# The low part of the second half of every weight piece on GpSimd instead of VectorE

## The chip, the cores and the metric

The kernel runs on one core of one Trainium2 chip. The metric is the device time of one execution in microseconds (us), the median over several runs. Five engines work side by side, each in the order of its own queue: TensorE (PE in the profile, with its weight loads as PEld), VectorE (DVE), ScalarE (ACT), GpSimd (POOL) and SyncE (SP), which here only issues DMAs.

## What is computed

The reference is two transformer-like blocks in float32 over 256 tokens of width 1024. The first block has four layers: a Fourier mixer, a grouped-query attention, a dilated attention and a Fourier mixer again, each with an input projection, a gate, an attention over 256 memory tokens, an output projection and a layer norm. The second block has two layers; each has an RMS norm, a mixer of three parts (a gated unit, a state-space part, a low-rank attention), an output projection, another RMS norm and an MLP with 4096 hidden units.

```python
proj = jnp.matmul(h, w_in_a[j])                # a 1024 x N projection in each layer
y = jnp.matmul(y.astype(h.dtype), w_out[i])
h = layer_norm(DEEPNORM_ALPHA * h + y, ln_g[i], ln_b[i])
...
x = x + mix @ w_out[l]
x = x + squared_relu_mlp(rmsnorm(x, norm_mlp_g[l]), mlp_w1[l], mlp_w2[l])
```

## The kernel before, in words

All weights lie in one array of 380 pieces of 128 partitions by up to 1024 columns, in the order of their use (`plan`, L30). A piece is loaded by SP into one of four `raw` buffers (`load_raw`, L117). Every float32 operand of a matrix product is split into a high part, rounded to the type fp32r, and a low part, the difference from it; a product is three matmuls (high by high, high by low, low by high; `Group.add`, L212). The weights are split on the fly, half a piece at a time (`split_w`, L149): ACT rounds the half into `wh` (L158), then VectorE subtracts it from `raw` into `wl` (L160). There are 12 buffers for `wh` halves and 12 for `wl` halves, so the split can run up to six pieces ahead of the matmuls; `W` (L177) asks for it two pieces ahead in the program. The manual dependence at L163 to L166 keeps a half behind the half two before it; since the halves alternate, that is the same half of the piece before.

The order of the instructions on each engine is set by a planner that goes by dependences, by the place in the program and by `high_priority`. Two hand-written orders matter. `late` (set at L345) and `tail_of_chain` (L142) put some low parts behind the last instruction of a norm on VectorE, `normed`: `issue_after` queues what is issued on the engine of that instruction behind it, and only that. The norms themselves run from the sum into `x` (L623, L1295, L1429) over statistics (L414, L419, or ACT's squares at L355) to two small POOL instructions (L289 and L290 in `rsqrt`, L360 and L361 in `rms_x`), then back to VectorE (L423 and L425, or L369) and by PE transposes (L298) into the halves `xTh` and `xTl` (L189, L190) that feed the next projections. The two halves of the tokens (`hf`) go through this one after the other.

Apart from the norms, POOL adds the two products of the rotary embedding (L200), makes the low part of the gated branch (L197), and issues a few DMAs (L686, L695, L910, L914).

Of the kernel before, what the change touches and what calls it, by code (L numbers as in the profile page):

```python
# [9 lines left out]
F32 = mybir.dt.float32  # L10
# [3 lines left out]
ALU = mybir.AluOpType  # L14
# [56 lines left out]
def used(key):  # L71

    return 512 if key.startswith("dftt") else width(key)
# [3 lines left out]
def kernel(ctx: ExitStack, tc: tile.TileContext, x_in, wall, vec, tabs, small, out, dbg=None):  # L77
    nc = tc.nc
    V, A, G, PE = nc.vector, nc.scalar, nc.gpsimd, nc.tensor
# [23 lines left out]
    def pt(shape, dt=F32):  # L103
        return ab.tile(shape, dt, tag="P", name="pt", bufs=4)
# [37 lines left out]
    def tail_of_chain():  # L142
        late["skip"] -= 1
        if late["skip"] < 0 and late["n"] > 0:
            late["n"] -= 1
            return tc.issue_after(late["after"])
        return ExitStack()

    def split_w(n):  # L149
        key, _ = order[n]  # L150
        w, t = used(key), raws.pop(n)
        cut = w // 2
        hs, ls = [], []
        for c in (slice(0, cut), slice(cut, w)):
            k = c.stop - c.start
            h = wp.tile([P, PC // 2], F32R, tag="wh", name="wh", bufs=NW)
            l = wp.tile([P, PC // 2], F32R, tag="wl", name="wl", bufs=NW)
            ih = A.copy(out=h[:, :k], in_=t[:, c]).ins  # L158
            with tail_of_chain():
                il = V.tensor_tensor(out=l[:, :k], in0=t[:, c], in1=h[:, :k].bitcast(F32), op=ALU.subtract).ins  # L160
            splits.append((ih, il))

            if len(splits) > HOLD:  # L163
                for i, before in zip((ih, il), splits[-1 - HOLD]):
                    tc.add_manual_dep(i, before.name, mybir.DependencyInfo(
                        mybir.DependencyClass.Sync, mybir.DependencyReason.DATA))  # L166
            hs.append(h)
            ls.append(l)
        wts[n] = (Halves(hs, cut), Halves(ls, cut))
# [7 lines left out]
    def W(key, i, ahead=AHEAD):  # L177
        n = where[(key, i)]
        while state["split"] <= min(n + ahead, len(order) - 1):
            while state["raw"] <= min(state["split"] + 1, len(order) - 1):  # L180
                load_raw(state["raw"])
                state["raw"] += 1
            split_w(state["split"])
            state["split"] += 1
        return wts[n]
# [258 lines left out]
    for i in range(4):  # L444
# [3 lines left out]
        for c in range(2):  # L448
            for kk in range(2):
                k = 2 * i + kk  # L450
# [467 lines left out]
    for hf in range(2):  # L918
        t = pt([P, 512])
# [13 lines left out]
    def ph2(shape, dt=F32R):  # L933
        return p2.tile(shape, dt, tag="ph2", name="ph2", bufs=12)
# [503 lines left out]
    for hf in range(2):  # L1438
        t = [ph2([P, 512], F32) for _ in range(2)]
# [3 lines left out]
        for b in range(2):  # L1443
            c = slice(b * 512, (b + 1) * 512)
# [169 lines left out]
```

## Time and profile before

| what | value |
|---|---|
| three runs | 1343.18 us median (1342.47 to 1346.27) |
| the profiled execution | 1345.01 us, span 1343.3 us |
| PE busy | 1281.3 us, 95% |
| VectorE busy | 981.2 us, 73% |
| ScalarE busy | 759.9 us, 57% |
| GpSimd busy | 179.3 us, 13% |
| mean granted TensorE clock | 0.979 of full speed |

A busy time counts every stretch in which the engine works on at least one instruction; the ends of matmuls are modelled. An idle time is put down to what ended it.

### The profile page before, as it was taken

The page shows a single profiled execution, that of the slowest core. Times are in us where ns is not written, and L with a number is a line of the kernel's source. Part 1 is how long each engine was busy: PE and PEld are TensorE (multiplying, and loading weights), DVE is VectorE, ACT ScalarE, POOL GpSimd, SP SyncE. Part 2 cuts the span into 40 slices and gives each one's busy share as a digit, 9 for nine tenths or more (in the row PEclk, how much of TensorE's full clock was granted, in tenths as well). Part 3 has the DMA queues.
Part 4 walks back from the last instruction along what each step waited for, and adds up shares of the span by engine and source line. Part 5 has one row for each costly group of instructions (what it writes and reads, how often), then busy time and mean ns, then how long its engine had stood idle before and what let it go on. Part 6 is the DMA issues. An engine that isn't in the chain of part 4 may idle for free. (4 is left out here: it accounts for less than half of the span.)

```text
span 1343.3 us, 21990 instructions
## 1 busy us (share of the span) xinstructions
PE 1281.3 (95%) x7620; PEld 1103.7 (82%) x7620; DVE 981.2 (73%) x1990; ACT 759.9 (57%) x1691; POOL 179.3 (13%) x290
## 2 busy tenths in 40 slices
PE   8999989899999999998998989999999998999997
PEld 6987868588788878897987887889898896789896
DVE  7788977788777777777777896765556897665654
ACT  5664576655555655663654784555454774554543
POOL 1132401111112111123032201000001201000000
PEclk9999999999899999998998998999999998999999
DMA  8574523354344434455554542565554552466561
GB/s 290 180 224 138 170 85 100 105 189 155 104 125 151 156 111 127 147 168 168 183 179 155 180 135 80 169 204 181 187 183 148 158 166 81 141 206 187 187 187 51
DMA packets 64063, 209.55 MB, mean 156 GB/s; under 512 B 8520, under 2 KB 10192, under 8 KB 63952
## 3 DMA queue, kind: packets, MB, share of 16 engines
q1 hardware_dynamic: 60480, 203.33, 47.8%
q0 software_dynamic: 1888, 3.15, 0.8%
q10 hardware_dynamic: 1584, 1.67, 0.4%
q8 instruction: 60, 0.98, 0.3%
q14 instruction: 51, 0.42, 0.1%
HBM read 204.97 MB, written 2.10 MB: 154 GB/s over the span
## 5 line engine op out<-in xcount | busy, mean ns | idle before, releaser
L160 DVE TENSOR_TENSOR wl<-raw,wh 128x512 fp32r<-128x512 f32 (+4 forms) x760 | 504.9, 690 | 195.9 <-ACT wh L158 191.2
L158 ACT CAST wh<-raw 128x512 fp32r<-128x512 f32 (+4 forms) x760 | 443.6, 606 | 299.9 <-issue 77.9
L217 PE MATMUL acc<-wh,ph 128*128 128x512 f32 (+2 forms) x672 | 224.2, 390 | 5.3 <-DVE pt L1315 1.7
L217 PE MATMUL acc<-wh,xTh 128*128 128x512 f32 (+3 forms) x560 | 218.8, 392 | 2.9 <-ACT xTh L189 1.3
L217 PE MATMUL acc<-wl,xTh 128*128 128x512 f32 (+3 forms) x560 | 217.5, 389 | 3.6 <-DVE wl L160 3.6
L217 PE MATMUL acc<-wh,xTl 128*128 128x512 f32 (+3 forms) x560 | 216.7, 389 | 3.3 <-DVE xTl L190 3.3
L217 PEld LDWEIGHTS acc<-wh,ph 128*128 128x128 f32 x672 | 125.9, 190 | 33.8 <-ACT ph L189 2.9
L217 PE MATMUL acc<-wl,ph 128*128 128x512 f32 (+2 forms) x336 | 131.2, 391 | 0.0
L217 PEld LDWEIGHTS acc<-wh,xTl 128*128 128x128 f32 x560 | 107.4, 192 | 24.0 <-DVE xTl L190 5.9
L217 PE MATMUL tp<-xTl,wh 128*128 128x256 f32 x448 | 126.6, 283 | 0.0
L217 PE MATMUL tp<-xTh,wl 128*128 128x256 f32 x448 | 126.6, 283 | 0.0
L217 PE MATMUL tp<-xTh,wh 128*128 128x256 f32 x448 | 126.6, 283 | 0.0
L217 PEld LDWEIGHTS acc<-wh,xTh 128*128 128x128 f32 x560 | 107.5, 192 | 22.5 <-ACT xTh L189 2.9
L217 PEld LDWEIGHTS acc<-wl,xTh 128*128 128x128 f32 x560 | 107.7, 192 | 21.7 <-DVE wl L160 4.3
L217 PE MATMUL sc<-wh,ph 128*128 128x512 f32 (+1 forms) x328 | 104.2, 369 | 0.0
L217 PE MATMUL acc<-xTh,wh 128*128 128x256 f32 x336 | 97.2, 290 | 0.0
L217 PE MATMUL acc<-xTh,wl 128*128 128x256 f32 x336 | 96.6, 288 | 0.0
L217 PE MATMUL acc<-xTl,wh 128*128 128x256 f32 x336 | 96.1, 286 | 0.0
L200 POOL TENSOR_TENSOR t<-t,t 128x256 f32<-128x256 f32 (+3 forms) x84 | 54.3, 672 | 244.6 <-DVE t L716 214.9
L217 PEld LDWEIGHTS tp<-xTl,wh 128*128 128x128 f32 x448 | 85.7, 191 | 0.5
L217 PEld LDWEIGHTS tp<-xTh,wh 128*128 128x128 f32 x448 | 85.5, 191 | 0.6
L217 PEld LDWEIGHTS tp<-xTh,wl 128*128 128x128 f32 x448 | 85.7, 191 | 0.0
(272 smaller groups left out, 2169.8 us busy)
## 6 DMA issues: line engine op xcount, KB each, us to landing
raw<-in_wall_dram SPq DMA_DIRECT2D x338, 512.0 KB, 4.1
raw<-in_wall_dram SPq DMA_DIRECT2D x20, 384.0 KB, 3.6
ph<-in_vec_dram SPq DMA_DIRECT2D x20, 256.0 KB, 6.5
raw<-in_wall_dram SPq DMA_DIRECT2D x8, 422.0 KB, 3.5
gn<-in_vec_dram SPq DMA_DIRECT2D x5, 512.0 KB, 4.7
raw<-in_wall_dram SPq DMA_DIRECT2D x6, 288.0 KB, 3.2
raw<-in_wall_dram SPq DMA_DIRECT2D x6, 256.0 KB, 3.0
x<-in_x_in_dram SPq DMA_DIRECT2D x2, 512.0 KB, 7.9
```

Source lines behind the costliest of these rows:

```text
L158: ih = A.copy(out=h[:, :k], in_=t[:, c]).ins
L160: il = V.tensor_tensor(out=l[:, :k], in0=t[:, c], in1=h[:, :k].bitcast(F32), op=ALU.subtract).ins
L200: G.tensor_tensor(out=out, in0=a, in1=b, op=ALU.add)
L217: done[0] = PE.matmul(out=self.out, lhsT=s, rhs=m, start=(i == 1), stop=(i == bk["n"]), skip_group_check=True).ins
```

## The change

The low part of the second half of a piece (`c.start` is not 0) is issued on GpSimd (`G`), that of the first half stays on VectorE (`V`). Operands, buffers and manual dependences stay as they are. There are 380 pieces, so 380 of the 760 subtractions move.

```diff
             ih = A.copy(out=h[:, :k], in_=t[:, c]).ins
             with tail_of_chain():
-                il = V.tensor_tensor(out=l[:, :k], in0=t[:, c], in1=h[:, :k].bitcast(F32), op=ALU.subtract).ins
+                il = (G if c.start else V).tensor_tensor(
+                    out=l[:, :k], in0=t[:, c], in1=h[:, :k].bitcast(F32), op=ALU.subtract).ins
             splits.append((ih, il))
```

## Rows read from the trace of the kernel before

**Rows 1.** Busy time, share of the span and instructions of each engine.

```profile
PE 1281.3 (95%) x7620; PEld 1103.7 (82%) x7620; DVE 981.2 (73%) x1990; ACT 759.9 (57%) x1691; POOL 179.3 (13%) x290
```

**Rows 2.** PE's waits: engine, line, waited for: us in total, times, longest.

```profile
PE sc L298 <- DVE pt L369: 5.6, 2, 3.7
PE sc L886 <- POOL t L200: 4.7, 2, 2.4
PE tp L528 <- DVE PTl L190: 4.5, 2, 2.2
PE acc L217 <- DVE wl L160: 3.8, 3, 3.4
PE sc L298 <- DVE x L425: 3.3, 3, 1.6
PE acc L217 <- DVE xTl L190: 3.3, 5, 0.9
...
PE pv L217 <- DVE PTl L190: 2.2, 6, 0.9
...
PE acc L217 <- DVE pt L1315: 1.7, 2, 1.0
...
PE acc L217 <- ACT ph L539: 1.4, 1, 1.4
...
PE tp L528 <- DVE pt L574: 1.2, 2, 0.6
```

**Rows 3.** Stretches: length, busy (instructions) PE, PEld, DVE, ACT, POOL, clock, DMA.

```profile
617.00:727.00 110.00, 99.41 (x584) 86.97 (x583) 83.47 (x157) 56.55 (x137) 27.61 (x43) 0.92 0.52 163
...
857.00:1024.00 167.00, 167.00 (x1047) 150.13 (x1045) 95.83 (x148) 84.23 (x150) 0.12 (x1) 1.00 0.59 185
```

**Rows 4.** Waits of ACT and of SP's queue for the weight pieces.

```profile
ACT wh L158 <- PE acc L217: 76.6, 76, 5.9
...
ACT wh L158 <- DMA raw<-in_wall_dram: 23.8, 16, 4.8
...
SPq L121 <- DVE wl L160: 956.7, 313, 24.3
```

**Rows 5.** VectorE's groups by shape: the commonest low part; busy, mean ns.

```profile
L160 DVE TENSOR_TENSOR wl<-raw,wh 128x512 fp32r<-128x512 f32 x676 | 462.2, 710 | 181.5 <-ACT wh L158 177.4
```

**Rows 6.** POOL's timeline: start, us; two-input instructions at 85, 256 and 818 us.

```profile
85.26 5.80 POOL L197 TENSOR_TENSOR ph<-sg,ph 128x256 fp32r<-128x256 f32 x5
...
256.35 1.43 POOL L197 TENSOR_TENSOR ph<-sg,ph 128x256 fp32r<-128x256 f32 x2 [15.09 <-ACT ph L539]
...
818.60 1.00 POOL L200 TENSOR_TENSOR y<-y,pt 128x384 f32<-128x384 f32 x1 [16.91 <-DVE pt L1279]
```

**Rows 7.** VectorE's timeline beside the first of those rows.

```profile
86.93 1.23 DVE L160 TENSOR_TENSOR wl<-raw,wh 128x512 fp32r<-128x512 f32 x1
```

**Rows 8.** Timelines of POOL, VectorE and ACT in the norm of 705 to 713 us.

```profile
705.18 0.53 POOL L289 TENSOR_SCALAR st<-st 128x1 f32<-128x1 f32 x1 [15.73 <-DVE st L419]
705.79 0.95 POOL L290 TENSOR_TENSOR st<-st,mhalf 128x1 f32<-128x1 f32 x1
...
706.90 1.41 DVE L425 SCALAR_TENSOR_TENSOR x<-x,st,ph 128x512 f32<-128x512 f32 x2
711.44 1.41 DVE L369 SCALAR_TENSOR_TENSOR pt<-x,st,gn 128x512 f32<-128x512 f32 x2 [3.13 <-POOL st L361]
...
705.18 3.41 ACT L158 CAST wh<-raw 128x422 fp32r<-128x422 f32 x5 [0.15 <-PE acc L217]
```

**Rows 9.** VectorE's timeline in the norm of 613 to 617 us.

```profile
614.84 0.69 DVE L160 TENSOR_TENSOR wl<-raw,wh 128x512 fp32r<-128x512 f32 x1
615.45 0.75 DVE L425 SCALAR_TENSOR_TENSOR x<-x,st,ph 128x512 f32<-128x512 f32 x1
616.11 0.69 DVE L160 TENSOR_TENSOR wl<-raw,wh 128x512 fp32r<-128x512 f32 x1
616.71 0.75 DVE L425 SCALAR_TENSOR_TENSOR x<-x,st,ph 128x512 f32<-128x512 f32 x1
```

**Rows 10.** The page's group of POOL's rotary additions.

```profile
L200 POOL TENSOR_TENSOR t<-t,t 128x256 f32<-128x256 f32 (+3 forms) x84 | 54.3, 672 | 244.6 <-DVE t L716 214.9
```

## The prediction

> **What bounds the kernel now.** I read the engines' busy times first: PE is busy for 1281.3 of 1343.3 us [rows 1]. What an edit on VectorE or POOL can win is therefore in the 62 us in which PE stands still; what it can lose has no such limit. Next come PE's waits, which say who ended those pauses. No single wait is large: VectorE's last multiplication of a norm (L369) 5.6 us, its low parts of attention weights 4.5 and 2.2 us, the rotary sums of POOL 4.7 us, and the low parts of the weights, the ones that the edit touches, 3.8 us in three places out of 760 [rows 2]. So PE almost never waits for a low part. The reason is in the split's own waits: ACT waited 76 times, 76.6 us in all, until PE's accumulations gave a weight buffer back, and only 16 times for a load [rows 4]. The split mostly runs as far ahead as the buffers let it. The stretches show where the pauses are: in the MLP from 857 to 1024 us PE is busy throughout, in the crossing from one block to the other (617 to 727 us) it is idle for 10.6 of 110 us [rows 3]. The end of a norm is where a few microseconds on VectorE, ACT or POOL become microseconds of the whole. A change to the low parts must be judged there.
>
> **The change part by part.**
>
> *What VectorE gives away.* 380 subtractions leave it. One takes 0.69 us undisturbed [rows 9] and 0.71 on average [rows 5]; the instructions start 0.6 us apart when they follow each other (614.84, 615.45) [rows 9]. That is 380 x 0.6 = 228 us less for an engine that is busy 73% of the time. It is off PE's path nearly everywhere, so by itself it brings little; what it can bring is in the rows of PE's waits that end on VectorE in the middle of a stage (4.5 + 2.2 + 1.7 + 1.2 = 9.6 us) [rows 2]. These chains run through ACT and PE too, so I take a third, **-3 us**; bounds 0 and -9.6.
>
> *What POOL takes on.* No low part of 512 columns has run there. Two subtractions of 256 columns took 1.43 us, 0.72 each, and one addition of 384 columns 1.00 us [rows 6]. 128 columns more cost 0.28, so 512 should take about 1.28 us, and 380 of them at most 486 us. POOL goes from 179 us [rows 1] to some 660, half the span; it is no bound by its sum. Per piece PE is busy for 1281.3 / 380 = 3.4 us, POOL for 1.28 more than now.
>
> *What the two engines do to each other.* This is the term that speaks most against the change. From 85.26 us POOL made five subtractions of 256 columns in 5.80 us, 1.16 each instead of 0.72 [rows 6], and beside them a low part on VectorE took 1.23 us instead of 0.69 [rows 7, 9]. Each held the other up: the rows read as two instructions that take turns at reading two SBUF operands. VectorE lost 0.54 us to a subtraction of 256 columns; with 256 more at 0.28 per 128 that is 0.54 + 0.56 = 1.10 us for one of 512. The Trainium skill (SBUF — State Buffer, "Who interferes with whom") states that a VectorE instruction with two SBUF inputs contends with a GpSimd instruction that reads SBUF, and that the loser waits for the whole instruction; the trace agrees on the contention, not on the whole instruction, since 0.54 is less than 0.72. By the page a hit would cost 1.28 instead of 1.10, which would add 1 us to the sum below.
>
> *The norms.* PE's work crosses seven norms between layers: after each of the four first layers, after both mixers of the second block and between its two layers. In each, the first half of the tokens has PE waiting at once. Three things happen.
> (a) The two small POOL instructions (705.18 and 705.79) come when VectorE has the statistics [rows 8]. In just that time ACT rounds weights, five halves from 705.18 on [rows 8], and every second one now calls POOL for 1.28 us. Whoever comes in between waits for what is left, half of it on average, 0.64 us. The order that keeps low parts behind a norm acts on VectorE's queue alone, so POOL's low parts are not held back. 7 x 0.64 = **+4.5 us**; lower bound 0, upper 14 half norms x 1.28 = 18.
> (b) L423, L425 and L369 read two SBUF operands (`x` with the weights of the norm). A layer norm has four of them per half, an RMS norm two. I count two hits in each of the four layer norms and one in each of three RMS norms, 11 hits of 0.55 us, half of 1.10: **+6.1 us**; lower bound 0, upper 7 x 3 low parts x 1.10 = 23, since five halves on ACT bring at most three to POOL.
> (c) A low part stands between the instructions of the chain: at 614.84, which runs while VectorE would wait anyway, and at 616.11, which doesn't [rows 9]. Where the second kind is a second half it goes: 7 x 0.6 = **-4.2 us**; bounds 0 and twice that.
>
> *POOL's other work.* The 84 rotary additions, in 42 pairs [rows 10], and the low parts of the branch queue behind weights. PE already waits for POOL's sums twice, 4.7 us, and once for the branch [rows 2]. There each delay shows at once: 3 x (0.64 + 0.44, the contention of the rows above) = **+3.3 us**. Lower bound 0; if every pair were late by 0.64 with no cover, 27. A low part on POOL that waits for ACT, as on VectorE (177.4 us of idle time before it [rows 5]), also holds back POOL's DMAs at the end of the dilated layer (L910, L914); their data are wanted a layer later, which hides it.
>
> *Loads.* SP waits for the last reader of a `raw` buffer, 313 times a low part [rows 4]. The second half now frees it 1.28 - 0.69 = 0.59 us later. Where the split is far ahead this is hidden; if that cover is gone, each load costs 0.59. ACT waited for a load 16 times [rows 4], at the start and just behind norms: 16 x 0.59 = 9.4 as the upper bound, 0 as the lower; most loads there wait for the transfers of their neighbours, so I take **+2 us**. The broadcasts of norm weights in SP's queue move by the same 0.59, ahead of a need that is several pieces away.
>
> *The MLPs.* PE stood still for nothing there and POOL was empty (0.12 us of work) [rows 3]: 0.
>
> Sum: -3 + 4.5 + 6.1 - 4.2 + 3.3 + 2 = **+8.7 us**. The profiled execution took 1345.0 us, so 1353.7; it lies 1.8 us above the median of the three runs, and against that median the forecast is **1352 us**. About 0.3% (4 us) is what a measurement of this kernel can tell from no change.
>
> **The rivals.**
> *VectorE is the better for it.* Its place is the norm and the attention chains: fewer low parts in VectorE's queue, and POOL's are done early because nothing holds them back, so behind a norm VectorE has two halves to make where it had four. For it: eight of the waits of PE shown end on VectorE, 5.6 + 4.5 + 3.8 + 3.3 + 3.3 + 2.2 + 1.7 + 1.2 = 25.6 us [rows 2]. Against: the contention in the rows above takes back more than it gives (1.10 against 0.6 us) wherever the two meet. Price: with a third of the 25.6 us won and (a), (b) and POOL's delays near nothing, 1343.2 - 8.5 = 1335 us. It decides where a hit is met in fewer than half the norms, so that what leaves the chain outweighs what is put in its way. Chance 0.20.
> *All is hidden.* The split is ahead, PE is never without work, and gains and losses at the norms cancel: 1343 us. For it: 3.8 us of waits for 760 low parts. Against: the norm chain, where nothing is ahead. Chance 0.18.
> *POOL's queue becomes the wait.* The planner puts a low part between the two small instructions of a norm, as the low parts stand between the instructions of VectorE's chain [rows 9], and rotary sums come late in most groups. Price: (a) with both a rest and a whole low part, 7 x (0.64 + 1.28) = 13.4 instead of 4.5, and 10 us more from rotary sums, half of their upper bound less what is counted: 1352 + 8.9 + 10 = 1371 us. The granted clock, 0.92 of 2.4 GHz in the crossing with pauses against 1.00 in the MLP [rows 3], would fall with longer pauses. Chance 0.17.
> That the edit does nothing is excluded: `c.start` is 0 for the first slice alone.
>
> **How the numbers follow.** The forecast has a chance of 0.45. Slower by over 0.3%: 0.45 + 0.17 = 0.62; within 0.3%: 0.18; faster: 0.20. The case of slower holds 0.62; its own range is 1347 to 1372. To hold 8 in 10 the range takes in the case of no change and the nearer half of the faster one, and reaches to the price of the third rival: **1338 to 1372 us**.
>
> **What would show it.** VectorE's busy time should fall to some 800 us (981 less 228 plus hits), POOL's rise to about 660 us or somewhat more with contention; low parts on POOL at 1.28 us alone and up to 1.8 in turns with VectorE; low parts on VectorE often over 1 us. In the norms the small POOL instructions should start later behind VectorE's statistics, and L425 and L369 should last over 0.75 us each. PE's waits for L369, L425 and POOL's sums should grow by some 10 us together, the MLPs stay free of waits. The forecast is wrong if PE's idle time outside the norms changes by more than 5 us, or if PE comes to wait for low parts in the middle of a stage.

## The result and the profile after

The changed kernel takes 1382.67 us (median of four runs, 1381.35 to 1384.44) against 1342.83 us of the kernel before beside it: a ratio of 1.0282, 95% interval 1.0267 to 1.0297, or 39.8 us more. The forecast of slower was right, its size was not: it said 1352 us, with a range up to 1372, and the measured time lies 10.7 us above that range. In the code of the change every line behind L160 has a number one higher than before (L425 is now L426, L369 is L370, L217 is L218).

The page of the changed kernel answers to [rows 1]; its profiled span is 1382.7 us:

```profile
PE 1298.8 (94%) x7620; PEld 1114.3 (81%) x7620; DVE 876.3 (63%) x1610; ACT 760.9 (55%) x1691; POOL 679.7 (49%) x670
...
L160 POOL TENSOR_TENSOR wl<-raw,wh 128x512 fp32r<-128x512 f32 (+4 forms) x380 | 518.4, 1364 | 482.4 <-ACT wh L158 336.1
...
L160 DVE TENSOR_TENSOR wl<-raw,wh 128x512 fp32r<-128x512 f32 (+4 forms) x380 | 333.3, 877 | 283.2 <-ACT wh L158 276.1
```

VectorE's busy share fell from 73% to 63%, POOL's rose from 13% to 49%, and no engine but PE is near its limit. Yet the kernel is slower. The last row has the first sign of why: a low part that stayed on VectorE now takes 877 ns on average over all shapes, against 690 ns on the page before:

```profile
L160 DVE TENSOR_TENSOR wl<-raw,wh 128x512 fp32r<-128x512 f32 (+4 forms) x760 | 504.9, 690 | 195.9 <-ACT wh L158 191.2
```

The multiplications of the norms, which also read two SBUF operands, by shape, the last ones of a norm first before:

```profile
L425 DVE SCALAR_TENSOR_TENSOR x<-x,st,ph 128x512 f32<-128x512 f32 x20 | 14.3, 748 | 2.7 <-POOL st L290 2.7
...
L369 DVE SCALAR_TENSOR_TENSOR pt<-x,st,gn 128x512 f32<-128x512 f32 x16 | 11.3, 748 | 8.8 <-POOL st L361 8.8
```

Then the same after, with the first multiplications of a layer norm (L424) and one more group:

```profile
L828 DVE TENSOR_SCALAR pt<-pt,st 128x512 f32<-128x512 f32 x32 | 26.3, 821 | 0.5
...
L426 DVE SCALAR_TENSOR_TENSOR x<-x,st,ph 128x512 f32<-128x512 f32 x20 | 21.4, 1110 | 3.6 <-POOL st L291 3.6
...
L370 DVE SCALAR_TENSOR_TENSOR pt<-x,st,gn 128x512 f32<-128x512 f32 x16 | 20.1, 1294 | 7.5 <-POOL st L362 7.5
...
L424 DVE SCALAR_TENSOR_TENSOR x<-x,st,ph 128x512 f32<-128x512 f32 x20 | 15.4, 811 | 0.4
```

L426 and L370 end every norm, and PE waits for them; they went from 748 ns to 1110 and 1294. L424 was 749 before. L828 scales the attention weights of the dilated layer; it reads one array and a column of factors, not two arrays, and yet it went from 484 to 821 ns. So the multiplications of the norms are not the only work that is held up. PE's waits after (us in total, times, longest), to be laid beside [rows 2]:

```profile
PE sc L299 <- DVE pt L370: 9.3, 5, 3.8
PE sc L299 <- DVE x L426: 8.2, 7, 1.6
PE acc L218 <- DVE wl L160: 7.3, 5, 4.3
PE acc L218 <- ACT ph L190: 5.2, 3, 3.9
PE acc L218 <- ACT ph L540: 4.8, 3, 3.6
PE sc L887 <- POOL t L201: 4.7, 2, 2.3
```

The first three are longer than before, nearly all of it behind norms; the wait for the sums of POOL (L887) is as long as before. The longest wait for `ph` at L190, 3.89 us, is at 151.62 us, at the start of an attention layer. The stretches (length, busy of PE, PEld, DVE, ACT, POOL, clock, DMA) answer to [rows 3]:

```profile
640.00:760.00 120.00, 104.83 (x607) 91.35 (x606) 79.97 (x137) 59.57 (x144) 64.99 (x78) 0.91 0.53 170
892.00:1058.00 166.00, 166.00 (x1040) 149.33 (x1039) 64.38 (x91) 84.53 (x151) 74.88 (x59) 1.00 0.57 182
```

The MLP is without a pause although POOL is now busy for 74.88 us in it; the crossing between the blocks has 15.2 us of pauses in 120.

**Where the 39.4 us of span went.** PE's idle time is span less busy: 1343.3 - 1281.3 = 62.0 before, 1382.7 - 1298.8 = 83.9 after, **21.9 us** more. PE's busy time grew from 1281.3 to 1298.8 us for the same 7620 instructions, the other **17.5 us**. The mean granted clock fell from 0.979 to 0.968. By it the part of the span that the clock took away is about 1343.3 x 0.021 = 28.2 us before and 1382.7 x 0.032 = 44.2 after, 16.0 us more, so the clock accounts for nearly all of the longer busy time. The loss is pauses, and a slower clock.

**One norm from close by.** The first layer norm before, VectorE's timeline (start, us, engine, line, operation; idle before and what ended it):

```profile
114.57 1.42 DVE L425 SCALAR_TENSOR_TENSOR x<-x,st,ph 128x512 f32<-128x512 f32 x2 [0.45 <-POOL st L290]
115.90 1.89 DVE L160 TENSOR_TENSOR wl<-raw,wh 128x512 fp32r<-128x512 f32 x3
```

The same place after, on VectorE, then on POOL and on ACT:

```profile
119.35 3.42 DVE L426 SCALAR_TENSOR_TENSOR x<-x,st,ph 128x512 f32<-128x512 f32 x2 [0.44 <-POOL st L291]
122.69 3.43 DVE L160 TENSOR_TENSOR wl<-raw,wh 128x512 fp32r<-128x512 f32 x2
```

```profile
117.54 0.75 POOL L290 TENSOR_SCALAR st<-st 128x1 f32<-128x1 f32 x1 [5.30 <-DVE st L420]
118.38 0.94 POOL L291 TENSOR_TENSOR st<-st,mhalf 128x1 f32<-128x1 f32 x1
119.29 6.29 POOL L160 TENSOR_TENSOR wl<-raw,wh 128x512 fp32r<-128x512 f32 x4
```

```profile
112.32 2.64 ACT L158 CAST wh<-raw 128x512 fp32r<-128x512 f32 x4 [0.17 <-POOL st L291]
```

ACT had rounded its halves by 114.96 us. POOL stood idle for 5.30 us before 117.54 and did not start on them: it ran them behind the norm's small instruction L291. That instruction ends at 119.3 and releases two things at once: VectorE's last multiplications (119.35) and POOL's whole row of low parts (119.29, four in 6.29 us, 1.57 each; alone one takes 1.29). The two engines meet where PE has little else to do. Two multiplications take 3.42 us in place of 1.42, 1.00 more each, and the two low parts behind them, which PE wants next, 3.43 in place of 1.89 for three.

What PE does then, by stretches: first before, then after.

```profile
114.40:120.00 5.60, 4.91 (x25) 3.61 (x24) 5.43 (x9) 1.18 (x2) 0.14 (x1) 1.00 0.30 89
120.00:126.10 6.10, 6.10 (x29) 5.05 (x28) 4.85 (x10) 2.85 (x6) 0.36 (x2) 1.00 0.84 255
```

```profile
119.20:125.00 5.80, 2.16 (x11) 1.34 (x10) 5.62 (x4) 1.17 (x2) 5.57 (x5) 0.87 0.00 1
125.00:131.00 6.00, 6.00 (x17) 4.61 (x16) 3.62 (x5) 0.28 (x2) 0.58 (x1) 0.55 0.77 227
151.60:158.60 7.00, 6.98 (x18) 5.53 (x19) 3.84 (x8) 0.39 (x2) 6.71 (x8) 0.57 0.45 146
```

Before, PE was busy for 4.91 of 5.60 us in the norm and the clock stayed at 1.00, the level of 2.4 GHz. After, it was busy for 2.16 of 5.80 us, and in the 6 us behind, busy throughout, the granted clock was 0.55: nearly all at the level of 1.2 GHz. PE's timeline shows what that is in matmuls:

```profile
125.09 0.63 PE L218 MATMUL acc<-wh,xTl 128*128 128x512 f32 x1
125.52 0.63 PE L218 MATMUL acc<-wh,xTh 128*128 128x512 f32 x1
...
131.22 0.39 PE L218 MATMUL acc<-wh,xTl 128*128 128x512 f32 x1
131.45 0.39 PE L218 MATMUL acc<-wh,xTh 128*128 128x512 f32 x1
```

One matmul starts 0.43 us after the other, later 0.23. In 6.0 us at a clock of 0.55 about 6.0 x 0.45 = 2.7 us more are lost. The third of those stretches, behind PE's wait at the start of the attention layer, loses about as much: 7.00 x 0.43 = 3.0 us.

### The profile page after: what moved, and what is told of

Same layout as the page of the kernel before. It is cut to its first block, busy times and chain, and to the rows that moved or that the text cites. A ratio compares the mean times of both kernels' runs of the same rounds, so it can differ in the third digit from the quotient of the medians.

```text
span 1382.7 us, 22197 instructions
## 1 busy us (share of the span) xinstructions
PE 1298.8 (94%) x7620; PEld 1114.3 (81%) x7620; DVE 876.3 (63%) x1610; ACT 760.9 (55%) x1691; POOL 679.7 (49%) x670
## 5 line engine op out<-in xcount | busy, mean ns | idle before, releaser
L160 POOL TENSOR_TENSOR wl<-raw,wh 128x512 fp32r<-128x512 f32 (+4 forms) x380 | 518.4, 1364 | 482.4 <-ACT wh L158 336.1
L160 DVE TENSOR_TENSOR wl<-raw,wh 128x512 fp32r<-128x512 f32 (+4 forms) x380 | 333.3, 877 | 283.2 <-ACT wh L158 276.1
L218 PE MATMUL acc<-wh,ph 128*128 128x512 f32 (+2 forms) x672 | 227.5, 394 | 10.6 <-ACT ph L540 4.8
L218 PE MATMUL acc<-wl,xTh 128*128 128x512 f32 (+3 forms) x560 | 222.6, 398 | 7.3 <-DVE wl L160 7.1
L218 PE MATMUL acc<-wh,xTh 128*128 128x512 f32 (+3 forms) x560 | 222.5, 399 | 5.5 <-ACT ph L190 3.9
L218 PE MATMUL acc<-wh,xTl 128*128 128x512 f32 (+3 forms) x560 | 219.8, 395 | 3.5 <-DVE xTl L191 3.5
L218 PEld LDWEIGHTS acc<-wh,ph 128*128 128x128 f32 x672 | 127.2, 192 | 40.6 <-ACT ph L540 6.1
L218 PE MATMUL acc<-wl,ph 128*128 128x512 f32 (+2 forms) x336 | 132.9, 396 | 0.3 <-POOL wl L160 0.3
L218 PEld LDWEIGHTS acc<-wl,xTh 128*128 128x128 f32 x560 | 110.3, 197 | 26.8 <-DVE wl L160 8.2
L218 PEld LDWEIGHTS acc<-wh,xTh 128*128 128x128 f32 x560 | 110.5, 197 | 25.2 <-ACT wh L158 4.1
L218 PEld LDWEIGHTS acc<-wh,xTl 128*128 128x128 f32 x560 | 110.0, 197 | 24.1 <-DVE xTl L191 6.1
L218 PE MATMUL tp<-xTl,wh 128*128 128x256 f32 x448 | 126.7, 283 | 0.0
L218 PE MATMUL tp<-xTh,wl 128*128 128x256 f32 x448 | 126.7, 283 | 0.0
L218 PE MATMUL tp<-xTh,wh 128*128 128x256 f32 x448 | 126.7, 283 | 0.0
L218 PE MATMUL sc<-wh,ph 128*128 128x512 f32 (+1 forms) x328 | 104.0, 369 | 0.0
L218 PE MATMUL acc<-xTh,wh 128*128 128x256 f32 x336 | 97.2, 289 | 0.0
L218 PE MATMUL acc<-xTh,wl 128*128 128x256 f32 x336 | 96.4, 288 | 0.0
L218 PE MATMUL acc<-xTl,wh 128*128 128x256 f32 x336 | 95.9, 286 | 0.0
L218 PEld LDWEIGHTS tp<-xTl,wh 128*128 128x128 f32 x448 | 85.7, 191 | 0.5
L218 PEld LDWEIGHTS tp<-xTh,wh 128*128 128x128 f32 x448 | 85.6, 191 | 0.6
L218 PEld LDWEIGHTS tp<-xTh,wl 128*128 128x128 f32 x448 | 85.7, 191 | 0.0
```

The lines of the kernel that those rows point to most:

```text
L160: il = (G if c.start else V).tensor_tensor(out=l[:, :k], in0=t[:, c], in1=h[:, :k].bitcast(F32), op=ALU.subtract).ins
L218: done[0] = PE.matmul(out=self.out, lhsT=s, rhs=m, start=(i == 1), stop=(i == bk["n"]), skip_group_check=True).ins
```

## Experiments

Three theories stood at the start: **A**, the loss sits at the norms, where VectorE's chain meets POOL's low parts; **B**, each moved low part costs the same (39.8 / 380 = 0.10 us); **C**, the planner makes another order of the whole program, and parts of the edit don't add up. Every ratio below is against the kernel before, run on the same chip in the same session (1343.84 to 1345.16 us), so that differences rather than times are to be compared.

**1. Which layers.** The move for one group of pieces only: the MLPs' 128, the dilated attention's 84, the other 168.

```diff
-                il = (G if c.start else V).tensor_tensor(
+                il = (G if c.start and key[0] == "m" and key != "memT" else V).tensor_tensor(   # the MLPs
+                il = (G if c.start and key == "c" else V).tensor_tensor(                        # the dilated layer
```

The third kernel has the negation of both conditions.

> Low parts of second halves go to GpSimd only in the pieces of the MLPs (m1, m2: 128 of 380). Theory A (the time is lost at the norms and in the attention that follows, where the chain on VectorE and GpSimd has no cover, and PE's clock falls after the pauses): about 1343 us, at most 4 more for the pieces at the norms beside the MLPs. Theory B (each moved low part costs a bit anywhere, by the later release of its raw buffer and the contention): 128/380 of 39.8 us, so about 1356. Theory C (the planner's new order of the instructions does it, not the engines' times): no figure, anything between.

> Low parts of second halves go to GpSimd only in the pieces of the dilated layer's projections (c: 84 of 380). Theory A: 1340 to 1350; the pieces behind the norm of the layer before cost up to 7 us, the middle of the layer gains 1 to 2, as the times at which PE first uses each piece show for the changed kernel. Theory B: 84/380 of 39.8, so about 1352. Theory C: open.

> Low parts of second halves go to GpSimd in all pieces but those of the MLPs and of the dilated layer's projections (168 of 380). Theory A: nearly the whole loss, 1375 to 1383 us. Theory B: 168/380 of 39.8, so about 1361. Together with the two others: the three losses should add up to 39.8 if stages are independent; a large remainder speaks for theory C.

MLPs: 1.0026 [1.001, 1.0042], +3.5 us. Dilated layer: 1.0059 [1.004, 1.0078], +7.7. The rest: 1.0202 [1.0179, 1.0224], +27.4. The sum is 38.6 against 39.8: the parts add up, which speaks against C. By B the MLPs would have cost 128 x 0.105 = 13.4 us; they cost a quarter of that, and 24 of their 128 pieces lie at norms. The dilated layer speaks the other way: 1352.9 us is above the 1340 to 1350 of A and at the 1352 of B. The rest, 1372.6, lies below A's 1375 and far above B's 1361. So B falls as the whole account, and A is not yet shown.

**2. Near the norms or away from them.** A piece is near where it is one of the eight ahead of a norm or of the eight behind it (112 pieces for seven norms, 268 others).

```diff
+    ends = [i + 1 for i, (k, _) in enumerate(order[:-1]) if order[i + 1][0] != k
+            and (k[0] in "op" or order[i + 1][0] == "cq1")]
+    near = {i + d for i in ends for d in range(-8, 8)}
...
-                il = (G if c.start else V).tensor_tensor(
+                il = (G if c.start and n not in near else V).tensor_tensor(   # away
+                il = (G if c.start and n in near else V).tensor_tensor(       # near
```

> The change everywhere but in the eight pieces before and the eight behind each of the seven norms between layers (112 pieces stay on VectorE, 268 low parts move). Theory A: 1345 to 1355, since the norms lose what they lose now and what is left is the attention of the second layer, the Fourier layer and the mixers. Theory B: 268/380 of 39.8, so about 1371.

> The opposite of the run away from norms: only the 112 pieces within eight of the seven norms between layers have the low part of their second half on GpSimd. If the places are independent, 39.8 less the 2.3 us (0.2%) that the 268 other pieces cost there: about 1380 us. If the loss comes from many moved low parts acting together, clearly less.

Away: 1.0022 [1.0009, 1.0034], +2.3 us for 268 low parts. Near: 1.028 [1.0259, 1.0301], +38.3 us for 112. Nearly the whole loss is in the 112. This also answers what VectorE's relief is worth: with 268 subtractions off it, nothing was won.

**3. Contention or queue.** Two kernels in which VectorE keeps all its work, and POOL gets work for nobody near the norms: a subtraction on a tile of its own, or two memsets of the same total length. Both wait for the half that ACT rounds, as a low part would; nothing waits for either.

```diff
+            if c.start and n in near:
+                ig = G.tensor_tensor(out=idle[:, :k], in0=idle[:, :k], in1=idle[:, :k], op=ALU.subtract).ins
+                tc.add_manual_dep(ig, ih.name, ...)
```

```diff
+            if c.start and n in near:
+                for _ in range(2):
+                    ig = G.memset(idle[:, :k * 5 // 4], 0.0).ins
+                    tc.add_manual_dep(ig, ih.name, ...)
```

> The kernel before, with an added GpSimd subtraction of the same width behind each rounding of a second half in those 112 pieces; it reads and writes a tile of its own, twice the same operand, and nobody waits for it. All low parts stay on VectorE, and no raw buffer is held. Contention theory (VectorE's two-operand instructions and GpSimd's take turns at reading SBUF): 25 to 50 us over the kernel before, as much as the near-norms run or more, since VectorE gives nothing away. Queue theory (norms and rotary sums wait in GpSimd's queue): also 25 to 40. Timeliness theory (PE lacks the low part or its load itself): under 5.

> As the run before, with two memsets of GpSimd, together about as long as one subtraction of 512 columns, in place of the added subtraction: GpSimd's queue is as full, but nothing is read. Contention theory: under 10 us over the kernel before. Queue theory: 25 to 40, as with the subtraction.

The subtractions: 1.0301 [1.0276, 1.0326], +41.1 us. The memsets: 1.0026 [1.0015, 1.0037], +3.9 us. The groups by shape, of the kernel with subtractions and then of the one with memsets:

```profile
L433 DVE SCALAR_TENSOR_TENSOR x<-x,st,ph 128x512 f32<-128x512 f32 x20 | 19.6, 1010 | 5.4 <-POOL st L298 5.4
...
L377 DVE SCALAR_TENSOR_TENSOR pt<-x,st,gn 128x512 f32<-128x512 f32 x16 | 15.7, 1020 | 7.4 <-POOL st L369 7.4
...
L164 POOL TENSOR_TENSOR idle<-idle 128x512 f32<-128x512 f32 x101 | 128.5, 1272 | 354.2 <-ACT wh L160 352.3
```

```profile
L434 DVE SCALAR_TENSOR_TENSOR x<-x,st,ph 128x512 f32<-128x512 f32 x20 | 14.3, 747 | 3.6 <-POOL st L299 3.6
...
L378 DVE SCALAR_TENSOR_TENSOR pt<-x,st,gn 128x512 f32<-128x512 f32 x16 | 11.3, 748 | 9.6 <-POOL st L370 9.6
...
L165 POOL MEMSET idle<- 128x640 f32 x202 | 128.2, 635 | 338.2 <-ACT wh L160 330.8
```

POOL is busy with them for the same time in both, 128.5 and 128.2 us in the commonest shape, behind the same halves of ACT. Where it reads SBUF, VectorE's multiplications go from 748 to 1010 and 1020 ns, and the kernel loses what the change loses. Where it only writes, they stay at 747 and 748. The two engines do meet in both kernels. In the first norm, POOL and VectorE with the subtractions, then with the memsets:

```profile
113.66 3.93 POOL L164 TENSOR_TENSOR idle<-idle 128x512 f32<-128x512 f32 x3
113.70 2.98 DVE L433 SCALAR_TENSOR_TENSOR x<-x,st,ph 128x512 f32<-128x512 f32 x2 [1.46 <-POOL st L298]
```

```profile
109.32 4.77 POOL L165 MEMSET idle<- 128x640 f32 x7
109.39 1.41 DVE L434 SCALAR_TENSOR_TENSOR x<-x,st,ph 128x512 f32<-128x512 f32 x2 [0.64 <-POOL st L299]
```

Beside the subtractions two multiplications take 2.98 us, beside the memsets 1.41. The small instructions of the norm are not what parts the two kernels: VectorE's last multiplications waited for them for 5.4 + 7.4 = 12.8 us in the first and 3.6 + 9.6 = 13.2 us in the second. So the loss near the norms is the contention of the two engines when POOL reads, about 41.1 - 3.9 = 37 us. What POOL's queue adds there by itself is at most the 3.9 us (2.0 to 5.0 by the interval). The Trainium skill (SBUF — State Buffer, "Who interferes with whom") states just this difference: a VectorE instruction with two SBUF inputs contends with a GpSimd instruction that reads SBUF, not with one that only writes. Both runs agree with it.

**4. Is it the place in POOL's queue?** The low parts of POOL are put behind POOL's last small instruction of the norm, so that none of those asked for behind the first half's norm can stand ahead of it.

```diff
+            with (pool_tail() if c.start else tail_of_chain()):   # issue_after POOL's power of the norm
```

> The change with GpSimd's low parts kept behind its own last instruction of the norm: from the first half of the tokens on all of them behind that half's power, then four behind the second half's power. Queue theory: the small instructions of the norms are late no more, 10 to 20 us less than the change, 1363 to 1373. Contention theory: the low parts meet VectorE's two multiplications behind the power all the more, within 5 us of the change, 1378 to 1388.

1.0304 [1.0285, 1.0323], +41.7 us: nothing won, as the contention theory expected. The groups show more meetings:

```profile
L437 DVE SCALAR_TENSOR_TENSOR x<-x,st,ph 128x512 f32<-128x512 f32 x20 | 25.6, 1317 | 2.4 <-POOL st L300 2.2
...
L381 DVE SCALAR_TENSOR_TENSOR pt<-x,st,gn 128x512 f32<-128x512 f32 x16 | 23.0, 1476 | 8.1 <-POOL st L373 8.1
```

In the layer norms the first small instruction now starts 0.1 us behind VectorE's statistics each time, and still more low parts begin together with the last multiplications (1317 and 1476 ns). Taken one by one from the trace, 27 of these 36 multiplications are held up by 0.2 us or more, against 18 of 36 in the change. The loss is the same within its interval, so it does not go by their number alone.

**5. Behind a norm, ahead of it, one norm alone, and a stretch without norms.**

```diff
-    near = {i + d for i in ends for d in range(-8, 8)}
+    near = {i + d for i in ends for d in range(8)}                             # behind
+    near = {i + d for i in ends for d in range(-8, 0)}                         # ahead
...
-                il = (G if c.start else V).tensor_tensor(
+                il = (G if c.start and 23 <= n < 39 else V).tensor_tensor(     # first norm alone
+                il = (G if c.start and key == "c" and 12 <= order[n][1] < 72 else V).tensor_tensor(   # middle of the dilated layer
```

> Of the 112 pieces near norms only the eight behind each of the seven norms (56 pieces) have the low part of their second half on GpSimd. The split runs up to six pieces ahead, so these are the ones that are split while the norm runs. Contention in the norm's chain: nearly the whole loss of the near-norms run (38.3 us), so 1372 to 1382 us. If the loss arises before the norm, in the attention and the output projection: under 1355.

> Only the eight pieces ahead of each norm (56 pieces). Contention in the norm's chain: 1343 to 1350 us, and with the run behind norms the two losses should add up to 38.3. If the loss arises before the norm: 1372 to 1382.

> Only the 16 pieces around the first of the norms between layers (8 ahead of it, 8 behind). If every norm pays for itself: 7 to 12 us, as much as the near-norms run had lost by the middle of the next layer. If the losses of the norms are a chain of one another: under 3.

> Only 60 pieces in the middle of the dilated layer's projections, away from any norm. In the changed kernel PE's use of these pieces came up to 2 us earlier against the kernel before than at the stage's start, so relief on VectorE: 1341 to 1343 us, 0.1% faster or no difference. If the relief was only the catching up of a delay: 1344 to 1346.

Behind: 1.0221 [1.0198, 1.0244], +29.8 us for 56 low parts. Ahead: 1.0083 [1.0064, 1.0103], +11.9, or 1355.7 us, which is in neither of the two ranges expected of it. The two sum to 41.7 against 38.3 of both together. PE's waits of the two kernels, behind and then ahead:

```profile
PE sc L301 <- DVE pt L372: 9.7, 6, 3.7
PE sc L301 <- DVE x L428: 8.3, 7, 1.7
PE acc L220 <- DVE wl L162: 7.0, 6, 4.3
```

```profile
PE sc L301 <- DVE pt L372: 6.3, 2, 3.7
...
PE sc L301 <- DVE x L428: 3.3, 3, 1.6
...
PE pv L220 <- ACT PTh L192: 3.6, 5, 1.4
...
PE pv L1182 <- DVE Bk L196: 3.1, 2, 1.5
```

The pieces behind a norm carry the waits of the change (9.7, 8.3 and 7.0 against 9.3, 8.2 and 7.3). With those ahead, the norm's waits are nearly as before, and PE waits in the attention that stands ahead of the output projection instead, for pieces of chains on ACT and VectorE that overlap with the split. The prediction had no term for that place. In this kernel the norm's multiplications keep their 746 to 748 ns, while the scaling of attention weights in the second block (L1172, 12 of 256 columns) goes from 403 to 747 ns. So the low parts ahead of a norm cost 11.9 us without touching its multiplications.

The first norm alone: 1.0065 [1.0048, 1.0082], +9.5 us for 16 low parts of 380. The middle of the dilated layer, 60 low parts and no norm: 0.9991 [0.9982, 1.0], 0.9 us less, no difference that can be told. It is the best version found, and it doesn't beat the kernel before.

**6. Moving the meeting.** First the low parts ahead of the norm in POOL's queue: the small instruction waits its turn behind the last low part asked for so far. Second, a wait: the low parts near a norm may start only when VectorE's last multiplication is done.

```diff
+    def behind_low():
+        return tc.issue_after(pooled[0]) if pooled[0] is not None else ExitStack()   # around the first small instruction
```

```diff
+            if c.start and hold["n"] >= 0:
+                tc.add_manual_dep(il, hold["after"].name, ...)   # hold["after"]: normed[0], the last multiplication
```

> The change with the norm's first small GpSimd instruction queued behind the last low part that the program has asked of GpSimd by then, instead of ahead of it. In the changed kernel GpSimd stood idle 5.3 us ahead of the second half's small instruction at 117.54 us and began four low parts as VectorE began its last two multiplications of the norm. If that meeting is a matter of the place in GpSimd's queue, the parts run in the idle time and the loss shrinks: 1355 to 1372 us. If the low parts meet the chain wherever they stand: 1378 to 1390.

> The change in which GpSimd's low parts asked for behind the first half's norm wait for VectorE's last multiplication of that norm to be finished, the first four behind the second half's norm for that of the second half. They can't meet the last multiplications. If these collisions alone make the loss, and the parts are not missed later: 1350 to 1365 us. If the low parts then come too late or meet VectorE's own low parts behind the norm, the loss only moves: 1375 or more.

The first: 1.0347 [1.0331, 1.0362], +46.1 us. It tells nothing of its question: the multiplications stayed at 1090 and 1296 ns, so the edit didn't move the meeting. Its time, 1391.2 us, is just above both ranges, and its further 6.3 us (46.1 - 39.8) were not followed up. The second: 1.0217 [1.0196, 1.0237], +29.1 us, between what the two theories expected. Its groups by shape and PE's longest wait:

```profile
L169 DVE TENSOR_TENSOR wl<-raw,wh 128x512 fp32r<-128x512 f32 x338 | 304.7, 901 | 265.3 <-ACT wh L167 258.1 <-issue 1.3 <-DVE wl L169 0.4
...
L440 DVE SCALAR_TENSOR_TENSOR x<-x,st,ph 128x512 f32<-128x512 f32 x20 | 15.6, 819 | 3.6 <-POOL st L303 3.6
...
L384 DVE SCALAR_TENSOR_TENSOR pt<-x,st,gn 128x512 f32<-128x512 f32 x16 | 12.2, 806 | 8.3 <-POOL st L376 8.3
```

```profile
PE acc L230 <- DVE xTl L203: 8.0, 6, 1.7
```

The multiplications are nearly back (819 and 806 ns), and 10.7 us with them (39.8 - 29.1). The mean clock of this run is 0.976, so the clock takes about 1372.0 x 0.024 = 32.9 us, 11.3 less than after the change; PE's idle time, 1372.0 - 1288.7 = 83.3, is as long as after the change. What was won back is thus clock, not pauses. What is left moved on: PE waits 8.0 us for the low part of the transposed activations (L203), which comes just behind the multiplications, and a low part of 512 columns on VectorE takes 901 ns, as long as after the change (894). So the last multiplications are a part of the loss, not the whole. By this reading the contention in the rest of VectorE's work is what remains, but no run isolates it.

## Why the prediction was right in direction and short in size

- **What bounds the kernel.** Right in the main. The change is judged near the norms: 112 low parts there cost 38.3 us, 268 elsewhere 2.3. The MLPs are without pauses, as forecast.
- **POOL's price.** Right: 1.29 us alone, 1.36 on average over all widths, 1.57 in turns; POOL busy for 679.7 us (some 660 or more forecast).
- **What VectorE gives away, -3 us.** Nothing: with 268 low parts off VectorE the time was +2.3 us. VectorE's busy time fell to 876 us, not 800, mainly because the low parts that stayed went from 690 to 877 ns, 380 x 0.187 = 71 us. The sum counts 228 us given away and has no such bill for the contention on the other half.
- **(a), small instructions late, +4.5, and the sums late, +3.3.** Mostly absent. VectorE's last multiplications waited for the small instructions for 2.7 + 8.8 = 11.5 us before and 3.6 + 7.5 = 11.1 after. PE's wait for the sums is 4.7 us, as before. PE's wait for the gate's branch (L540) did grow, from 1.4 to 4.8. Near the norms the kernel with memsets puts the queue at 3.9 us at most, against 7.8 forecast for these two terms. One place has what (a) and the third rival meant, the start of the attention layer on POOL's timeline:

```profile
141.26 1.79 POOL L160 TENSOR_TENSOR wl<-raw,wh 128x512 fp32r<-128x512 f32 x1
143.01 1.02 POOL L291 TENSOR_TENSOR st<-st,mhalf 128x4 f32<-128x4 f32 x1
```

The first small instruction (L290) ran at 139.40 us, and a low part ended late between the two. VectorE then waits 2.17 us for L291, and its two multiplications behind that take 2.94 us beside two more low parts; PE stands still for 3.89 us until 151.62 us.

- **(b), the contention, +6.1. This is the step that failed, by its size.** The mechanism was right: where POOL reads SBUF, VectorE is held up, and a full hit is 1.00 us in the first norm, 1.10 forecast. But the term was "11 hits of 0.55 us" on the multiplications of the norms, and every other instruction of VectorE was put at nothing. In its place the runs show about 37 us for POOL's reads near the norms (41.1 us with subtractions less 3.9 with memsets), the slower clock behind the pauses included. On the multiplications alone the groups give 20 x (1.110 - 0.748) + 16 x (1.294 - 0.748) + 20 x (0.811 - 0.749) = 7.2 + 8.7 + 1.2 = 17.2 us in place of 6.1. Taken one by one, 20 of these 56 are held up, by 0.2 to 1.1 us; 18 of the 20, 0.88 us each, are in the seven norms counted. So the count was too small, and so was half a hit for each. In the first norm the reason is plain: POOL's ready low parts stand behind the norm's small instruction and start in the same moment as the last multiplications, which is no chance meeting. The upper bound of 23 us held the 17.2, but not the term as a whole: in experiment 6, sparing most of the last multiplications gave back only 10.7 of the 39.8 us.
- **(c), low parts leaving the chain, -4.2.** Wrong in sign at the first norm: behind its multiplications two low parts of VectorE take 3.43 us where three took 1.89.
- **Loads, +2.** Not seen: ACT's waits for loads went from 23.8 us to 17.6.
- **A term that was missing.** The sum has none for the clock; it stands in the third rival alone. It is some 16 of the 39.4 us, within the loss above and not on top of it. In the two stretches shown, PE's wait is paid again behind it at a clock near 0.55.
- **PE's waits.** L370 +3.7, L426 +4.9, POOL's sums 0: 8.6 us, about the 10 forecast. But PE's whole idle time grew by 21.9. The waits behind the norms, for low parts, for the halves of the activations and for the branch, grew as well. One of the signs of being wrong came true: PE's idle time outside the norms was to change by less than 5 us. Between the first two norms it was 123.00 - 112.79 = 10.2 us before (135 to 258 us) and 132.90 - 116.91 = 16.0 us after (143.1 to 276 us, its counterpart by the number of PE's instructions), with the wait of 3.89 us in it.
- **The rivals.** "VectorE is the better for it" argued from 25.6 us of waits that end on VectorE; the contention took more, as the case against it said. "POOL's queue becomes the wait" came nearest with 1371 us, but for another reason than the loss has: near the norms the queue cost at most 3.9 us, POOL's reads about 37.

Open are three points: whether a place of POOL's low parts ahead of the norm would save the time (the run meant for it didn't move them); how the 29 us that stay with the multiplications spared divide between the low parts, the activations and the attention; and by which of the instructions held up in the attention the low parts ahead of a norm cost their 11.9 us.

## What to carry to other kernels

Before work moves from VectorE to GpSimd to relieve VectorE, ask whether both would then read SBUF at the same time: here VectorE's busy share fell by ten points and the kernel lost 2.8%. Count the hold-up on all that the relieved engine keeps, and not only on the chain looked at first. Look for what releases both: where one instruction frees the chain and a row of ready work on the other engine, the two meet by order and not by chance, and such a hit is to be counted in full. To part contention from the queue, put in work of the same length that only writes. Count a pause at a stage's end twice, once as the pause and once for the clock behind it, if the trace shows the granted clock falling there.

## What the runs showed of the hardware that was not expected

- The contention depends on reading: in the kernel with subtractions of POOL VectorE's multiplications went from 748 to 1010 and 1020 ns on average, in the one with memsets of the same total time they stayed at 747 and 748. It costs both sides: four low parts on POOL took 1.57 us each beside VectorE, 1.29 alone.
- It is not confined to instructions of VectorE with two arrays: the scaling L828, with one array and a column of factors, went from 484 to 821 ns after the change.
- A hit is shorter than the instruction that causes it: 1.00 us more per multiplication, beside low parts that take 1.29 us alone and 1.57 in turns.
- Behind a stretch in which PE was busy for 2.16 of 5.80 us, the next 6 us had a granted clock of 0.55; behind one with 4.91 of 5.60 us it stayed at 1.00. Sixteen low parts at one norm lengthened the multiplications by 20 x (0.846 - 0.748) = 2.0 us and the whole kernel by 9.5.
